# Average pooling over length 4: f32 loads without a cast, 512-row tiles, fewer buffers and a last tile in pieces

## Chip, cores and metric

The kernel runs on one core of a Trainium2 chip, with the other cores idle. The metric is the device time of one execution in microseconds (us), and a smaller time is better. The granted clock (of TensorE, which this kernel does not use) was 1.0 in every run.

## The reference

```python
x = randn(64, 256, 8192) as float32; kernel_size = 4; stride = 4
for i in range(2048):
    output[:, :, i] = mean(x[:, :, 4*i : 4*i + 4], axis=2)      # float32
```

Seen flat, 16384 rows of 8192 numbers (32 KB a row, 536.9 MB in all) become 16384 rows of 2048 numbers (8 KB a row, 134.2 MB). There is about one addition per number read, so the work is nearly all movement.

## The kernel before

```python
    P = nc.NUM_PARTITIONS
    assert num_rows % P == 0
    n_tiles = num_rows // P

    inv_k = 1.0 / float(k)

    f16 = mybir.dt.float16
    f32 = mybir.dt.float32

    with (
        nc.allow_low_precision(reason="fp16 pooling: DMA-bandwidth bound kernel"),
        tc.tile_pool(name="pin", bufs=3) as pin,
        tc.tile_pool(name="psum", bufs=3) as psum,
        tc.tile_pool(name="pout", bufs=3) as pout,
    ):
        for i in range(n_tiles):
            tin = pin.tile([P, out_len * k], f16, name="tin")
            nc.gpsimd.dma_start(
                out=tin, in_=x_flat[i * P : (i + 1) * P, 0 : out_len * k]
            )
            tsum = psum.tile([P, out_len], f16, name="tsum")
            nc.vector.reduce_sum(
                out=tsum,
                in_=tin.rearrange("p (g k) -> p g k", k=k),
                axis=mybir.AxisListType.X,
            )
            tout = pout.tile([P, out_len], f32, name="tout")
            nc.scalar.mul(tout, tsum, inv_k)
            nc.scalar.dma_start(out=out_flat[i * P : (i + 1) * P], in_=tout)

```

A tile is 128 rows, one in each partition. GpSimd issues the load; because the tile is f16 and the source f32, the transfer itself casts. VectorE sums groups of four, ScalarE multiplies by 1/4 and widens to f32, and ScalarE issues the store. Each pool has three buffers, so a load waits for the reduce three tiles before it. There are 128 such tiles; nothing is special about the first or the last. The launch code around it is left out here.

Of the kernel before, what the change touches and what calls it, by code (L numbers as in the profile page):

```python
# [1 line left out]

# [4 lines left out]


@with_exitstack
def kernel(  # L10
    ctx: ExitStack,
    tc: tile.TileContext,
    x: bass.AP,
    kernel_size: bass.AP,
    stride: bass.AP,
    out: bass.AP,
):
    nc = tc.nc

    k = int(kernel_size)  # L20
    s = int(stride)
    assert k == s, f"only kernel_size == stride supported (got {k}, {s})"

    x_flat = x.flatten_outer_dims()
    out_flat = out.flatten_outer_dims()
    num_rows, length = x_flat.shape
    out_len = out_flat.shape[1]
    assert out_len * k <= length

    P = nc.NUM_PARTITIONS  # L30
    assert num_rows % P == 0
    n_tiles = num_rows // P

    inv_k = 1.0 / float(k)

    f16 = mybir.dt.float16
    f32 = mybir.dt.float32

    with (
        nc.allow_low_precision(reason="fp16 pooling: DMA-bandwidth bound kernel"),  # L40
        tc.tile_pool(name="pin", bufs=3) as pin,
        tc.tile_pool(name="psum", bufs=3) as psum,
        tc.tile_pool(name="pout", bufs=3) as pout,
    ):
        for i in range(n_tiles):
            tin = pin.tile([P, out_len * k], f16, name="tin")
            nc.gpsimd.dma_start(  # L47
                out=tin, in_=x_flat[i * P : (i + 1) * P, 0 : out_len * k]
            )
            tsum = psum.tile([P, out_len], f16, name="tsum")  # L50
            nc.vector.reduce_sum(  # L51
                out=tsum,
                in_=tin.rearrange("p (g k) -> p g k", k=k),
                axis=mybir.AxisListType.X,
            )
            tout = pout.tile([P, out_len], f32, name="tout")
            nc.scalar.mul(tout, tsum, inv_k)  # L57
            nc.scalar.dma_start(out=out_flat[i * P : (i + 1) * P], in_=tout)


# [1 line left out]
_INS = ['x', 'kernel_size', 'stride']  # L62
_OUTS = [((64, 256, 2048), 'float32')]
#: Inputs that are plain numbers.
_NUMBERS = {'kernel_size': 4, 'stride': 4}


# [26 lines left out]
```

## Time and profile before

| | before |
|---|---|
| time, median of 13 runs | 1578.23 us (1578.12 to 1578.70) |
| span of the profiled run | 1576.4 us |
| DMA engines busy | nine tenths or more in 39 of 40 slices |
| VectorE / ScalarE busy | 71% / 16% |
| time of 512 rows (four tiles), steady | 48.81 us |

The last row is mine: from the timeline, the time from the start of a reduce to the start of the reduce four later, as the median over the run. I use 512 rows because that is one tile of the changed kernel. I call it the *step*.

These are lines of the profile page of the kernel before. Group lines give line, engine, operation, shapes and count, then busy us and mean ns of one, then the idle time of the engine before them and what ended it. Queue lines give packets, MB and share of the 16 engines' time. Issue lines give the median us from issue to landing.

```profile
span 1576.4 us, 937 instructions
...
DMA  9999999999999999999999999999999999999997
...
q0 software_dynamic: 18432, 268.44, 79.8%
q10 hardware_dynamic: 18432, 134.23, 21.0%
...
HBM read 536.87 MB, written 134.22 MB: 426 GB/s over the span
...
L51 DVE TENSOR_REDUCE tsum<-tin 128x2048 f16<-128x8192 f16 x128 | 1111.8, 8686 | 457.9 <-DMA tin<-in_x_dram 457.9
L57 ACT ACTIVATE tout<-tsum 128x2048 f32<-128x2048 f16 x128 | 244.4, 1909 | 1325.2 <-DVE tsum L51 1325.2
...
tin<-in_x_dram POOLq DMA_DIRECT2D x128, 2048.0 KB, 27.5
out_dram<-tout ACTq DMA_DIRECT2D x128, 1024.0 KB, 20.8
```

Read it from the DMA row: the engines never rest, and the two queues' shares (79.8% and 21.0%) add up to the whole span. VectorE's idle 457.9 us all end at a load. The load queue's 268.44 MB counts the f16 bytes that reach SBUF; the line "HBM read" counts the f32 bytes that leave HBM.

These are lines of the timeline of the kernel before: start us, duration us, engine, line, operation, and in brackets the idle time before it and its releaser. They show the first two reduces, two reduces four tiles apart in the steady part (one step), and the end.

```profile
13.78 8.69 DVE L51 TENSOR_REDUCE tsum<-tin 128x2048 f16<-128x8192 f16 x1 [13.78 <-DMA tin<-in_x_dram]
...
23.43 8.69 DVE L51 TENSOR_REDUCE tsum<-tin 128x2048 f16<-128x8192 f16 x1 [0.96 <-DMA tin<-in_x_dram]
...
1207.09 8.69 DVE L51 TENSOR_REDUCE tsum<-tin 128x2048 f16<-128x8192 f16 x1 [3.53 <-DMA tin<-in_x_dram]
...
1255.90 8.69 DVE L51 TENSOR_REDUCE tsum<-tin 128x2048 f16<-128x8192 f16 x1 [3.52 <-DMA tin<-in_x_dram]
...
1561.00 8.69 DVE L51 TENSOR_REDUCE tsum<-tin 128x2048 f16<-128x8192 f16 x1 [3.52 <-DMA tin<-in_x_dram]
1569.72 1.91 ACT L57 ACTIVATE tout<-tsum 128x2048 f32<-128x2048 f16 x1 [10.30 <-DVE tsum L51]
1571.66 0.34 ACTq L58 DMA_DIRECT2D out_dram<-tout  x1
```

The second tile is ready 9.65 us after the first, before any store has run: 4.194 MB of source in 9.65 us is 435 GB/s. After the last load lands at 1561.0, the reduce, the scaling and the store follow one after the other until 1576.4.

### The profile page before, as it was taken

To read this page: it belongs to the slowest core of one execution; us is meant where nothing else is said; L and a number is where in the kernel's file an instruction comes from. 1 tells how busy PE (TensorE), PEld (TensorE's weight loads), DVE (VectorE), ACT (ScalarE), POOL (GpSimd) and SP (SyncE) were. 2 spreads that over 40 slices of the span, in tenths; PEclk is the share of its full clock that TensorE was granted. 3 is DMA by queue.
4 is the path that set the end of the run, shared out by engine and by line. 5 is a ranking of instruction groups with operands and counts; after the bars stand their busy time and mean duration, and the time that the engine had idled before them with its cause. 6 is when DMAs were issued, how large, how long until landed. Compare 5 with 4: busy or idle time off the path is not lost.

```text
span 1576.4 us, 937 instructions
## 1 busy us (share of the span) xinstructions
DVE 1111.8 (71%) x128; ACT 245.7 (16%) x129; POOL 67.9 (4%) x132
## 2 busy tenths in 40 slices
DVE  5766777677766777677767776677767776677766
ACT  1111111111111111111111111111111111111111
POOL 0000000000000000000000000000000000000000
DMA  9999999999999999999999999999999999999997
GB/s 212 256 259 256 257 256 259 262 256 256 255 258 262 259 257 256 257 259 257 259 258 255 258 257 259 262 256 256 256 261 259 257 259 254 259 259 256 259 258 212
DMA packets 36871, 402.73 MB, mean 255 GB/s; under 512 B 4096, under 2 KB 4096, under 8 KB 4096
## 3 DMA queue, kind: packets, MB, share of 16 engines
q0 software_dynamic: 18432, 268.44, 79.8%
q10 hardware_dynamic: 18432, 134.23, 21.0%
q14 instruction: 7, 0.06, 0.0%
HBM read 536.87 MB, written 134.22 MB: 426 GB/s over the span
## 4 chain that ended last, share of the span: by engine, by line
DMA 75%; DVE 23%; issue 2%; ACT 0%; DVEq 0%; POOL 0%; POOLq 0%; PEldq 0%
DMA tin<-in_x_dram 75%; DVE tsum L51 23%; ACT tout L57 0%; DVEq L51 0%; POOL tin L47 0%; POOLq L89 0%; PEldq L89 0%; POOLq L47 0%
## 5 line engine op out<-in xcount | busy, mean ns | idle before, releaser
L51 DVE TENSOR_REDUCE tsum<-tin 128x2048 f16<-128x8192 f16 x128 | 1111.8, 8686 | 457.9 <-DMA tin<-in_x_dram 457.9
L57 ACT ACTIVATE tout<-tsum 128x2048 f32<-128x2048 f16 x128 | 244.4, 1909 | 1325.2 <-DVE tsum L51 1325.2
L47 POOL DMA_DIRECT2D tin<-in_x_dram x128 | 67.7, 529 | 1465.7 <-DVE tsum L51 1450.7
L57 ACT ACT_TABLE_LOAD x1 | 1.3, 1283 | 0.7 <-PEq L75 0.7
L75 POOL MEMSET const-float32-0.0<- 128x1 f32 x1 | 0.1, 99 | 0.2 <-issue 0.2
L75 POOL MEMSET const-bfloat16-1.0<- 128x1 bf16 x1 | 0.1, 102 | 0.0
L75 POOL MEMSET const-float32-1.0<- 128x1 f32 x1 | 0.1, 99 | 0.0
L75 POOL MEMSET const-uint8-127<- 128x1 uint8 x1 | 0.1, 99 | 0.0
## 6 DMA issues: line engine op xcount, KB each, us to landing
tin<-in_x_dram POOLq DMA_DIRECT2D x128, 2048.0 KB, 27.5
out_dram<-tout ACTq DMA_DIRECT2D x128, 1024.0 KB, 20.8
```

Source lines behind the costliest of these rows:

```text
L47: nc.gpsimd.dma_start(out=tin, in_=x_flat[i * P : (i + 1) * P, 0 : out_len * k])
L51: nc.vector.reduce_sum(out=tsum, in_=tin.rearrange("p (g k) -> p g k", k=k), axis=mybir.AxisListType.X,)
L57: nc.scalar.mul(tout, tsum, inv_k)
L75: nc = _bacc.Bacc("TRN2", target_bir_lowering=False, num_devices=1)
```

## The change

Its intent is to spend less on the transfers and their ends: no cast, larger transfers, a short tail. Four rows go to each partition (`(p q) l -> p (q l)`), so that a 512-row tile is loaded in two halves of 8.4 MB with 64 KB in one run per partition, and stored as one 4.2 MB transfer with 32 KB per partition. The input pool has two buffers of 64 KB per partition, the result pool two of 32 KB; the scaling is done in place. The last tile is loaded, reduced, scaled and stored by quarters, the last quarter by quarters again, and the store of the tile before it is held back behind the last loads.

```diff
-            tin = pin.tile([P, out_len * k], f16, name="tin")
-            nc.gpsimd.dma_start(
-                out=tin, in_=x_flat[i * P : (i + 1) * P, 0 : out_len * k]
-            )
...
+        with (
+            tc.tile_pool(name="pin", bufs=2) as pin,
+            tc.tile_pool(name="pq", bufs=2) as pq,
+        ):
+            for t in range(n_super):                 # 32 tiles of 512 rows, Q = 4
+                x_view = x_flat[R0 : R0 + super_rows].rearrange("(p q) l -> p (q l)", q=Q)
+                o_view = out_flat[R0 : R0 + super_rows].rearrange("(p q) m -> p (q m)", q=Q)
+                if t == n_super - 1:
...                     # by quarters j: load, reduce, scale, store; j == 3 in four pieces again
+                    continue
+                pqt = pq.tile([P, Q * out_len], f32, name="pq")
+                for h in range(Q // 2):
+                    tin = pin.tile([P, half_in], f32, name="tin")
+                    xh = x_view[:, h * half_in : (h + 1) * half_in]
...
+                    nc.sync.dma_start(out=tin, in_=xh)
+                    nc.vector.reduce_sum(out=pqt[:, h * half_out : (h + 1) * half_out],
+                                         in_=tin.rearrange("p (g k) -> p g k", k=k), axis=X)
+                nc.scalar.mul(pqt, pqt, inv_k)
+                if t == n_super - 2:
+                    deferred.append((o_view, pqt))
+                else:
+                    nc.scalar.dma_start(out=o_view, in_=pqt)
+            for o_view, pqt in deferred:
+                nc.sync.dma_start(out=o_view, in_=pqt)
```

(The lines are joined here, and a path for other shapes, which these inputs do not take, is left out.)

More of the change, by code (lines that the diff above doesn't have):

```diff
@@ L27 @@
     out_len = out_flat.shape[1]
-    assert out_len * k <= length
+    used_len = out_len * k
+    assert used_len <= length
     P = nc.NUM_PARTITIONS
+    inv_k = 1.0 / float(k)
+    f32 = mybir.dt.float32
+    X = mybir.AxisListType.X
+    Q = 4
+    super_rows = P * Q
+    fast = (
+        used_len == length
+        and num_rows % super_rows == 0
+        and out_len % 4 == 0
+        and length % (2 * k) == 0
+        and num_rows // super_rows >= 4
+    )
+    if fast:
+        n_super = num_rows // super_rows
+        half_in = 2 * length
+        half_out = 2 * out_len
+        with (
+            tc.tile_pool(name="pin", bufs=2) as pin,
+            tc.tile_pool(name="pq", bufs=2) as pq,
+        ):
+            deferred = []
+            for t in range(n_super):
+                R0 = t * super_rows
+                x_view = x_flat[R0 : R0 + super_rows].rearrange(
+                    "(p q) l -> p (q l)", q=Q
+                )
+                o_view = out_flat[R0 : R0 + super_rows].rearrange(
+                    "(p q) m -> p (q m)", q=Q
+                )
+                if t == n_super - 1:
+                    pqt = pq.tile([P, Q * out_len], f32, name="pq")
+                    for j in range(Q):
+                        if j % 2 == 0:
+                            tin2 = pin.tile([P, half_in], f32, name="tin")
+                        tinq = tin2[:, (j % 2) * length : (j % 2 + 1) * length]
+                        src = x_view[:, j * length : (j + 1) * length]
+                        oq = o_view[:, j * out_len : (j + 1) * out_len]
+                        if j < Q - 1:
+                            nc.sync.dma_start(out=tinq[:, 0:length], in_=src)
+                            nc.vector.reduce_sum(
+                                out=pqt[:, j * out_len : (j + 1) * out_len],
+                                in_=tinq[:, 0:length].rearrange(
+                                    "p (g k) -> p g k", k=k
+                                ),
+                                axis=X,
+                            )
+                            nc.scalar.mul(
+                                pqt[:, j * out_len : (j + 1) * out_len],
+                                pqt[:, j * out_len : (j + 1) * out_len],
+                                inv_k,
+                            )
+                            nc.scalar.dma_start(
+                                out=oq, in_=pqt[:, j * out_len : (j + 1) * out_len]
+                            )
+                        else:
+                            C = 4
+                            cin = length // C
+                            cout = out_len // C
+                            for c in range(C):
+                                nc.sync.dma_start(
+                                    out=tinq[:, c * cin : (c + 1) * cin],
+                                    in_=src[:, c * cin : (c + 1) * cin],
+                                )
+                                o_lo = j * out_len + c * cout
+                                o_hi = j * out_len + (c + 1) * cout
+                                nc.vector.reduce_sum(
+                                    out=pqt[:, o_lo:o_hi],
+                                    in_=tinq[:, c * cin : (c + 1) * cin].rearrange(
+                                        "p (g k) -> p g k", k=k
+                                    ),
+                                    axis=X,
+                                )
+                                nc.scalar.mul(
+                                    pqt[:, o_lo:o_hi], pqt[:, o_lo:o_hi], inv_k
+                                )
+                                nc.scalar.dma_start(
+                                    out=oq[:, c * cout : (c + 1) * cout],
+                                    in_=pqt[:, o_lo:o_hi],
+                                )
+                    continue
+                pqt = pq.tile([P, Q * out_len], f32, name="pq")
+                for h in range(Q // 2):
+                    tin = pin.tile([P, half_in], f32, name="tin")
+                    xh = x_view[:, h * half_in : (h + 1) * half_in]
+                    if t == 0 and h == 0:
+                        nc.sync.dma_start(out=tin, in_=xh)
+                    else:
+                        nc.sync.dma_start(out=tin, in_=xh)
+                    nc.vector.reduce_sum(
+                        out=pqt[:, h * half_out : (h + 1) * half_out],
+                        in_=tin.rearrange("p (g k) -> p g k", k=k),
+                        axis=X,
+                    )
+                nc.scalar.mul(pqt, pqt, inv_k)
+                if t == n_super - 2:
+                    deferred.append((o_view, pqt))
+                else:
+                    nc.scalar.dma_start(out=o_view, in_=pqt)
+            for o_view, pqt in deferred:
+                nc.sync.dma_start(out=o_view, in_=pqt)
+        return
@@ L31 @@
     assert num_rows % P == 0
     n_tiles = num_rows // P
-    inv_k = 1.0 / float(k)
-    f16 = mybir.dt.float16
-    f32 = mybir.dt.float32
     with (
-        nc.allow_low_precision(reason="fp16 pooling: DMA-bandwidth bound kernel"),
         tc.tile_pool(name="pin", bufs=3) as pin,
@@ L45 @@
         for i in range(n_tiles):
-            tin = pin.tile([P, out_len * k], f16, name="tin")
-            nc.gpsimd.dma_start(
-                out=tin, in_=x_flat[i * P : (i + 1) * P, 0 : out_len * k]
-            )
-            tsum = psum.tile([P, out_len], f16, name="tsum")
+            r0, r1 = i * P, (i + 1) * P
+            tin = pin.tile([P, used_len], f32, name="tin")
+            nc.sync.dma_start(out=tin, in_=x_flat[r0:r1, 0:used_len])
+            tsum = psum.tile([P, out_len], f32, name="tsum")
             nc.vector.reduce_sum(
@@ L53 @@
                 in_=tin.rearrange("p (g k) -> p g k", k=k),
-                axis=mybir.AxisListType.X,
+                axis=X,
             )
@@ L57 @@
             nc.scalar.mul(tout, tsum, inv_k)
-            nc.scalar.dma_start(out=out_flat[i * P : (i + 1) * P], in_=tout)
+            nc.scalar.dma_start(out=out_flat[r0:r1], in_=tout)
 _INS = ['x', 'kernel_size', 'stride']
```

## The prediction

> **What bounds the kernel now.** The 16 DMA engines. The page shows them at nine tenths or more in 39 of 40 slices; its queue part gives 79.8% of their time to loads and 21.0% to stores. VectorE is 71% busy; in the waits view VectorE waits for loads 128 times, 457.9 us. A steady tile takes 12.20 us in the timeline. The cast to f16 happens inside the load, so 4.19 MB leave HBM per tile though 2.1 MB reach SBUF; with the 1.05 MB store that is 5.24 MB in 12.20 us, 430 GB/s. Before any store ran, the second tile's data came 9.65 us after the first's (reduces start at 13.78 and 23.43): 435 GB/s of source bytes. The Trainium skill ("DMA: Bandwidth & Descriptors", Where 436 GB/s comes from) puts the ceiling at 435 GB/s; this trace agrees if source bytes are counted. So the engines are charged by HBM bytes: the cast saves them nothing.
>
> **What the change does.**
> - Drops the cast; f32 loads of 8.4 MB go from SyncE's queue instead of GpSimd's. HBM bytes stay: 536.9 MB in, 134.2 MB out. SBUF receives twice as much. I expect no change of rate.
> - Reduces: 62 of 128x16384 f32, plus a finer last tile. 8,686 ns for 8192 f16 columns is 1.06 ns a column; f32 should cost the same (the skill's "VectorE: DVE Perf Modes", tier table, caps the reduce at 1x for both): 17.2 us each. Off the chain.
> - Scaling: 31 large in-place ACTIVATEs, about 7 us each, scaled from 1,909 ns. Off the chain.
> - Stores: 4.2 MB in 32 KB rows instead of 1 MB in 8 KB rows. A store now costs 12.20-9.65 = 2.55 us (411 GB/s); larger pieces may lower it towards 2.41 us, saving up to 18 us in all.
> - Tail: now the last load lands at 1561.0 and 8.7 us of reduce, 1.9 of scaling and 3.9 of store follow, about 15 us, DMA mostly idle. After: quarter-pieces with reduce 2.3 us, scale 0.6, store about 2, while a held-back 4.2 MB store fills the DMA. Saves about 8 to 10 us.
>
> **Two buffers instead of three.** A load waits for the reduce two before it. That reduce (17.2 us) must end before the next load's data (19.3 us at 435 GB/s, no store running) do: about 2 us for semaphores and issue; stores widen it. The fastest store landed in 3.9 us against 2.4 of data: 1.5 us of latency, no bubble. If nearer 3 us, each of 31 tiles loses about 1 us.
>
> **Sum.** Loads 128 x 9.65 = 1235 us, stores 309 to 326, head about 3, tail about 3: 1550 to 1567 us. I predict **1564 us**, range **1547 to 1594**. Chances: faster by over 2%: 0.07; within 2%: 0.81; slower by over 2%: 0.12.
>
> **What would show it.** DMA at nine tenths or more in all slices, mean near 430 GB/s (the page's 255 now counts cast bytes); load queue near 79%; 48.8 us or less per 512-row tile; reduces near 17.2 us; the last load followed by about 10 us, filled by the held-back store; a chain of waits nearly all DMA.
>
> **What would make it wrong.** Writing SBUF at the full 435 GB/s could be slower; rows of one load at a 128 KB pitch could suit HBM worse; f32 reduces could run slower, closing the two-buffer slack; large stores could hold back loads; latency could open a bubble per tile.

## The result

| | before | after |
|---|---|---|
| time, median | 1578.23 us (13 runs) | 1557.73 us (7 runs, 1556.74 to 1561.30) |
| span of the profiled run | 1576.4 us | 1555.6 us |
| step (512 rows), median | 48.81 us | 48.33 us |
| reduce of 8192 columns a partition | 8.686 us | 8.61 us (half of 17.220) |

The ratio is 0.9877 (95% interval 0.9867 to 0.9887). A ratio is the mean time of one kernel's runs over that of the other's in the same rounds, so it is not quite the ratio of the medians. The class is "same" at 2%: 1.2% faster, and clear of the noise.

These are the lines of the profile page of the changed kernel that answer to those above.

```profile
span 1555.6 us, 418 instructions
...
DMA  9999999999999999999999999999999999999999
...
q1 hardware_dynamic: 10080, 541.07, 80.5%
q10 hardware_dynamic: 5328, 130.03, 19.4%
...
HBM read 536.87 MB, written 134.22 MB: 431 GB/s over the span
...
L125 DVE TENSOR_REDUCE pq<-tin 128x4096 f32<-128x16384 f32 x62 | 1067.6, 17220 | 443.4 <-DMA tin<-in_x_dram 443.4
L130 ACT ACTIVATE pq<-pq 128x8192 f32<-128x8192 f32 x31 | 217.9, 7030 | 1298.2 <-DVE pq L125 1298.2
...
out_dram<-pq ACTq DMA_DIRECT2D x30, 4096.0 KB, 32.9
...
tin<-in_x_dram SPq DMA_DIRECT2D x62, 31.1
```

It is the same picture: DMA full, VectorE waiting for loads, compute unchanged in cost. The bytes between HBM and SBUF moved at 431 GB/s in place of 426. (The load queue's 541.07 MB includes the one held-back store, which is issued from SyncE.)

These are lines of the timeline of the changed kernel in its steady part.

```profile
1418.97 17.22 DVE L125 TENSOR_REDUCE pq<-tin 128x4096 f32<-128x16384 f32 x1 [4.62 <-DMA tin<-in_x_dram]
...
1445.48 17.22 DVE L125 TENSOR_REDUCE pq<-tin 128x4096 f32<-128x16384 f32 x1 [9.28 <-DMA tin<-in_x_dram]
...
1467.32 17.22 DVE L125 TENSOR_REDUCE pq<-tin 128x4096 f32<-128x16384 f32 x1 [4.62 <-DMA tin<-in_x_dram]
```

The bracket is also the slack of the two buffers. A reduce ends, its buffer is free, and the next load into it can be issued at once; VectorE then waits 4.62 or 9.28 us for the load that is already on its way. So each load is queued that long before its predecessor lands, and the queue does not run dry.

These are lines of the stretches view at the end: start and end of the stretch, its length, busy us and instructions of VectorE, ScalarE and GpSimd, TensorE's clock, DMA share, GB/s. The kernel before:

```profile
1530.00:1561.00 31.00, 20.44 (x4) 5.73 (x3) 0.53 (x1) 1.00 1.01 266
1561.00:1570.00 9.00, 8.68 (x1) 0.28 (x1) 0.00 (x0) 1.00 0.25 106
1570.00:1576.00 6.00, 0.00 (x0) 1.63 (x1) 0.00 (x0) 1.00 0.42 175
```

The changed kernel:

```profile
1512.00:1537.00 25.00, 25.00 (x4) 10.07 (x4) 0.00 (x0) 1.00 0.99 420
1537.00:1546.00 9.00, 8.58 (x4) 4.03 (x5) 0.00 (x0) 1.00 1.05 450
1546.00:1551.00 5.00, 0.00 (x0) 0.24 (x1) 0.00 (x0) 1.00 0.92 391
1551.00:1555.60 4.60, 0.00 (x0) 0.00 (x0) 0.00 (x0) 1.00 0.58 222
```

Before, the DMA stood at a quarter for 9 us and under a half for 6 us. After, it is nearly full until about 1551. By these shares the DMA stood idle for about 10 us after the last load had landed, and for about 2.3 us after 1546 in the changed kernel: some 8 us less.

So the 20.8 us of span have two parts. The step fell by 0.48 us; over some 31 steps that is 15 us. The remaining 6 us are put down to head and tail together; that is 2 us less than the idle time that the tail alone lost, so the split is good to a few us only. The experiments ask which part of the change made which.

### The profile page after: what moved, and what is told of

The parts are those of the page before. It is cut to its first block, busy times and chain, and to the rows that moved or that the text cites. A ratio compares the mean times of both kernels' runs of the same rounds, so it can differ in the third digit from the quotient of the medians.

```text
span 1555.6 us, 418 instructions
## 1 busy us (share of the span) xinstructions
DVE 1102.2 (71%) x69; ACT 227.4 (15%) x39; POOL 0.2 (0%) x4
## 3 DMA queue, kind: packets, MB, share of 16 engines
q1 hardware_dynamic: 10080, 541.07, 80.5%
## 4 chain that ended last, share of the span: by engine, by line
DMA 63%; DVE 36%; issue 0%; DVEq 0%; ACT 0%; SPq 0%
DMA tin<-in_x_dram 63%; DVE pq L125 34%; DVE pq L75 2%; DVE pq L101 0%; DVEq L190 0%; ACT pq L108 0%; SPq L122 0%
## 5 line engine op out<-in xcount | busy, mean ns | idle before, releaser
L125 DVE TENSOR_REDUCE pq<-tin 128x4096 f32<-128x16384 f32 x62 | 1067.6, 17220 | 443.4 <-DMA tin<-in_x_dram 443.4
L130 ACT ACTIVATE pq<-pq 128x8192 f32<-128x8192 f32 x31 | 217.9, 7030 | 1298.2 <-DVE pq L125 1298.2
L75 DVE TENSOR_REDUCE pq<-tin 128x2048 f32<-128x8192 f32 x3 | 25.9, 8676 | 0.0
L101 DVE TENSOR_REDUCE pq<-tin 128x512 f32<-128x2048 f32 x4 | 8.9, 2276 | 0.0
L82 ACT ACTIVATE pq<-pq 128x2048 f32<-128x2048 f32 x3 | 5.7, 1910 | 14.9 <-DVE pq L75 14.9
## 6 DMA issues: line engine op xcount, KB each, us to landing
out_dram<-pq ACTq DMA_DIRECT2D x4, 256.0 KB, 10.8
```

What stands on the lines that cost most here:

```text
L75: nc.vector.reduce_sum(out=pqt[:, j * out_len : (j + 1) * out_len], in_=tinq[:, 0:length].rearrange("p (g k) -> p g k", k=k), axis=X,)
L82: nc.scalar.mul(pqt[:, j * out_len : (j + 1) * out_len], pqt[:, j * out_len : (j + 1) * out_len], inv_k,)
L101: nc.vector.reduce_sum(out=pqt[:, o_lo:o_hi], in_=tinq[:, c * cin : (c + 1) * cin].rearrange("p (g k) -> p g k", k=k), axis=X,)
L125: nc.vector.reduce_sum(out=pqt[:, h * half_out : (h + 1) * half_out], in_=tin.rearrange("p (g k) -> p g k", k=k), axis=X,)
L130: nc.scalar.mul(pqt, pqt, inv_k)
```

## The experiments

Twelve kernels ran. "Step" is the median step of the profiled run; times of timed runs are medians. The kernel before took 1578.17 us beside the first four, 1578.57 beside the next four and 1578.21 beside the last four, so times can be compared across them although the three groups ran on different chips.

| run | time, us | step, us |
|---|---|---|
| before | 1578.2 | 48.81 |
| after | 1557.73 | 48.33 |
| e1_f32_small: cast dropped, SyncE's queue | 1569.45 | 48.53 |
| e7_f32_pool: cast dropped, GpSimd's queue | 1570.26 | 48.54 |
| e4_before_tail: before, last tile in quarters | 1572.51 | 48.82 |
| e2_no_tail: after, without tail code | 1579.91 | 48.34 |
| e9_no_hold: after, store not held back | 1559.98 | 48.34 |
| e6_quarter_4buf: after, 4 MB loads, four buffers | 1565.87 | 48.50 |
| e3_small_stores: after, 1 MB stores | 1724.61 | not steady |
| e8_small_both: after, 1 MB stores, 2 MB loads | 1572.51 | 48.90 |

The other four move one kind of data only: l_cast 1252.34 us, l_f32 1255.30, s_1mb 327.96, s_4mb 325.59. All kernels of the table gave the correct result; these four are wrong.

### The cast alone: e1_f32_small and e7_f32_pool

Theory A was the prediction's: the engines are charged by HBM bytes, so dropping the cast is worth nothing. Theory B said that the cast and GpSimd's queue cost rate.

```diff
-            tin = pin.tile([P, out_len * k], f16, name="tin")
-            nc.gpsimd.dma_start(
+            tin = pin.tile([P, out_len * k], f32, name="tin")
+            nc.sync.dma_start(
...
-            tsum = psum.tile([P, out_len], f16, name="tsum")
+            tsum = psum.tile([P, out_len], f32, name="tsum")
```

> The kernel before with the cast dropped alone: f32 loads of 4 MB from SyncE's queue, three buffers, 1 MB stores and the old tail kept. Theory A (the engines are charged by HBM bytes, so cast and queue are worth nothing; the steady gain of the change is the larger stores): the steady tile stays at 12.20 us and the time is 1575 to 1579 us. Theory B (the cast and GpSimd's queue cost rate): the steady tile falls to about 12.08 us (a quarter of the 48.33 us of the changed kernel) and the time to about 1562 us.

It took 1569.45 us, between the two: 8.7 us were gained, ratio 0.9945 (0.9930 to 0.9959), and the step fell to 48.53 us. Theory A is wrong for the mixed case, and theory B does not get all of it. The next run puts the f32 loads back on GpSimd's queue.

```diff
-            nc.sync.dma_start(
+            nc.gpsimd.dma_start(
```

> The kernel with the cast dropped alone, but its f32 loads issued from GpSimd's queue as before. The run with SyncE's queue took 1569.45 us, the kernel before 1578.2. If the cast itself was the cost beside stores: about 1570 us and 48.6 us per 512 rows. If GpSimd's queue was: about 1578 us and 48.85 us.

It took 1570.26 us with a step of 48.54 us, ratio 0.9950 (0.9933 to 0.9966). So the steady gain is the cast's, not the queue's. SyncE's queue is worth another 0.8 us, and that is at the head: the first reduce starts at 13.11 us with it and at 13.89 us without. (Both edits also make the sums f32. The reduces and the scalings take 8,686 and 1,909 ns either way, so that is not where the gain comes from.) These two reduces of e1 are one step apart:

```profile
1273.32 8.69 DVE L51 TENSOR_REDUCE tsum<-tin 128x2048 f32<-128x8192 f32 x1 [3.44 <-DMA tin<-in_x_dram]
...
1321.85 8.69 DVE L51 TENSOR_REDUCE tsum<-tin 128x2048 f32<-128x8192 f32 x1 [3.43 <-DMA tin<-in_x_dram]
```

### Loads and stores by themselves: l_cast, l_f32, s_1mb, s_4mb

Each of these keeps the pools of the kernel before and drops everything but one kind of transfer (the loads keep one store at the end). Here with the cast; l_f32 has `f32` and `nc.sync` in those places:

```diff
         for i in range(n_tiles):
             tin = pin.tile([P, out_len * k], f16, name="tin")
             nc.gpsimd.dma_start(out=tin, in_=x_flat[...])
-            ... reduce, scale, store
+        tout = pout.tile([P, out_len], f32, name="tout")
+        nc.scalar.mul(tout, tin[:, 0:out_len], inv_k)
+        nc.scalar.dma_start(out=out_flat[0:P], in_=tout)
```

The stores alone, with Q = 1 (s_1mb) or Q = 4 (s_4mb):

```diff
-            ... load, reduce, scale, store
+        for t in range(n_tiles // Q):
+            tout = pout.tile([P, Q * out_len], f32, name="tout")
+            nc.vector.memset(tout, 0.0)
+            nc.scalar.dma_start(
+                out=out_flat[t * P * Q : (t + 1) * P * Q].rearrange("(p q) m -> p (q m)", q=Q),
+                in_=tout,
+            )
```

> Loads alone, f32 to f16 with the cast from GpSimd's queue, three buffers, one store at the end, result wrong on purpose. Theory A: 9.65 us a load, about 1235 us of loads and about 1245 us in all. If the engines were charged by the bytes that reach SBUF it would be half of that.

> Loads alone, f32 kept, from SyncE's queue, same sizes and buffers, result wrong on purpose. Theory A: the same as with the cast, 9.65 to 9.68 us a load, 1243 to 1248 us in all. Theory B (cast and software queue cost rate): clearly shorter than the run with the cast, by about 15 us.

> Stores alone, 128 of 1 MB with 8 KB rows from tiles set to zero, result wrong on purpose. If small pieces cost by themselves: 2.55 us each, about 330 us. If they cost only among loads: about 2.41 us each, 310 to 315 us.

> Stores alone, 32 of 4 MB with 32 KB rows from tiles set to zero, result wrong on purpose. About 2.41 to 2.43 us per MB-tile, 310 to 315 us; the difference to the run with 1 MB stores is what the piece size costs by itself, expected about 15 us.

The loads took 1252.34 us with the cast and 1255.30 us without: alone, the cast costs nothing that these show (it is even 3 us the shorter). (Both are at least 7 us above what I expected: the rate at the head, 9.65 us a load, does not quite hold.) These are the queue lines of the DMA view between 200 and 1200 us, first with the cast:

```profile
q0 software_dynamic: 14864, 216.54, 101.6%
```

and without it:

```profile
q1 hardware_dynamic: 14831, 431.99, 100.4%
```

In the same 1000 us the cast delivered 216.54 MB of f16 (433.1 MB of source) and the plain load 431.99 MB of f32. So the engines are indeed charged by HBM bytes when only loads run. The plain load takes 4.194/0.432 = 9.71 us per 128 rows; with the cast, the issues in the timeline stand 9.69 us apart.

The stores alone took 327.96 and 325.59 us in all, but the second run begins its first store only at 9.4 us, after a longer memset, so the totals hide the difference. These are the sums of the DMA view between 50 and 250 us, first with 1 MB stores (8 KB rows), then with 4 MB stores (32 KB rows):

```profile
DMA packets 11505, 83.78 MB, mean 419 GB/s; under 512 B 1279, under 2 KB 1279, under 8 KB 1279
```

```profile
DMA packets 2950, 86.18 MB, mean 431 GB/s; under 512 B 320, under 2 KB 320, under 8 KB 320
```

That is 2.50 and 2.43 us per 128 rows. Small stores do cost by themselves: 0.07 us, 9 us over 128 tiles, less than the 15 us that I had expected.

Now the parts can be summed, four tiles to a step:

| | sum of the parts | measured step |
|---|---|---|
| before: cast load + 8 KB rows | 4 x (9.69 + 2.50) = 48.76 | 48.81 |
| e1: plain load + 8 KB rows | 4 x (9.71 + 2.50) = 48.84 | 48.53 |
| e6: plain 4 MB load + 32 KB rows | 4 x (9.71 + 2.43) = 48.56 | 48.50 |

With the cast, loads and stores add up in full. Without it, loads and small stores together take 0.31 us less than their sum. By this sum, the gain of dropping the cast is overlap, which appears only where both directions run together. (The parts come from one look each, so the sum is an argument; that the gain is there, and is the cast's, e1 and e7 show.) Why the engines can overlap plain transfers a little and not casting ones, no run here shows.

### Large stores or large loads: e6_quarter_4buf

```diff
-            tc.tile_pool(name="pin", bufs=2) as pin,
+            tc.tile_pool(name="pin", bufs=4) as pin,
...
-                for h in range(Q // 2):
-                    tin = pin.tile([P, half_in], f32, name="tin")
-                    xh = x_view[:, h * half_in : (h + 1) * half_in]
+                for h in range(Q):
+                    tin = pin.tile([P, length], f32, name="tin")
+                    xh = x_view[:, h * length : (h + 1) * length]
...                     # and the reduce writes out_len columns at a time
```

(The last tile's quarters each get a buffer of their own too.)

> The changed kernel with f32 loads of 4 MB (32 KB rows) into four buffers in place of 8 MB (64 KB rows) into two: the same SBUF, more loads ahead; stores and tail kept. If two buffers cost nothing and only the bytes and the store pieces count: the period of 512 rows stays at 48.3 to 48.4 us and the time within 4 us of the changed kernel, 1554 to 1562 us. If two large buffers open a bubble: at least 10 us faster than the changed kernel. If the 64 KB load rows are what gained: the period goes back to 48.6 us and the time to about 1565 us.

It took 1565.87 us (1564.13 to 1567.10), ratio 0.9921 (0.9906 to 0.9936), with a step of 48.50 us. The time is that of the third case of the expectation; the step lies between the first and the third. These two reduces of e6 are one step apart:

```profile
1204.56 8.69 DVE L123 TENSOR_REDUCE pq<-tin 128x2048 f32<-128x8192 f32 x1 [10.68 <-DMA tin<-in_x_dram]
...
1253.06 8.69 DVE L123 TENSOR_REDUCE pq<-tin 128x2048 f32<-128x8192 f32 x1 [10.70 <-DMA tin<-in_x_dram]
```

The difference to e1's step, 48.53, is 0.03 us although the stores are four times as large. The difference to the changed kernel, 48.33, is 0.17 us although only the form of the loads differs. So the large stores by themselves gave next to nothing, and the part of the steady gain that is not the cast's came with the loads in halves of 8.4 MB. (The large stores are needed all the same: with small ones, these loads lose far more, as e3 below shows.) The loads differ in three ways at once (row length, transfer size, number of buffers), and which of the three counts stays open; no run has the large loads by themselves. Four buffers of half the size gave no gain: two were enough. The 8 us between the two kernels are no measure of the loads alone. The profiled run of e6 has a stretch of steps of 49.2 to 50.2 us, which the median hides: its mean step from the third to the 31st tile is 48.76 us, against 48.36 in the changed kernel and 48.58 in e1. And its tail is worse: in its last 11.3 us the DMA share is 0.30, in the last 4.6 us of the changed kernel 0.58.

### The tail: e4_before_tail, e2_no_tail, e9_no_hold

e4_before_tail gives the kernel before a last tile in quarters:

```diff
-        for i in range(n_tiles):
+        for i in range(n_tiles - 1):
...
...                     # i, cin, cout and the three tiles of the last 128 rows
+        for c in range(4):
+            a, b = slice(c * cin, (c + 1) * cin), slice(c * cout, (c + 1) * cout)
+            nc.gpsimd.dma_start(out=tin[:, a], in_=x_flat[i * P : (i + 1) * P, a])
+            nc.vector.reduce_sum(out=tsum[:, b], in_=tin[:, a].rearrange("p (g k) -> p g k", k=k), axis=X)
+            nc.scalar.mul(tout[:, b], tsum[:, b], inv_k)
+            nc.scalar.dma_start(out=out_flat[i * P : (i + 1) * P, b], in_=tout[:, b])
```

> The kernel before with only its last tile cut into four quarter-length pieces (load, reduce, scale, store each), cast kept. Expected from its own durations: 6.4 us less of reduce, 1.3 less of scaling and about 1.5 less of store after the last load, so 1568 to 1572 us with a steady tile of 12.20 us. If the idle DMA at the end is not what the tail costs, it stays above 1575 us.

It took 1572.51 us, 5.7 less than before, ratio 0.9964 (0.9949 to 0.9978), at an unchanged step of 48.82 us. That is just outside the range that I gave, and in its direction: VectorE had work left over when the last quarters came (its four short reduces run back to back from 1557.07), so the saving was smaller than the sum of durations.

e2_no_tail takes the tail code out of the changed kernel:

```diff
-                if t == n_super - 1:
+                if False:
...
-                if t == n_super - 2:
+                if False:
```

> The changed kernel with its special last tile and held-back store taken out: the last 512 rows are handled like the others. Both theories: steady period unchanged at 48.33 us. After the last load come 17.2 us of reduce, 7.0 of scaling and about 11 of store, and the store of the tile before covers only the first few us of it, so about 20 us of idle DMA are added: 1572 to 1582 us, which would eat the whole gain of the change. If the tail is worth little, it stays below 1563 us.

It took 1579.91 us, ratio 1.0014 (0.9997 to 1.0030), with the step of the changed kernel (48.34). These are its last stretches:

```profile
1541.00:1550.00 9.00, 8.42 (x1) 0.00 (x0) 0.00 (x0) 1.00 0.14 58
1550.00:1566.00 16.00, 8.80 (x1) 7.03 (x1) 0.00 (x0) 1.00 0.00 0
1566.00:1577.80 11.80, 0.00 (x0) 0.00 (x0) 0.00 (x0) 1.00 0.83 355
```

The DMA does nothing for 16 us while 17.2 us of reduce and 7.0 us of scaling finish, and then a 4.2 MB store runs alone. A four times larger tile makes a longer tail, and that alone eats the whole gain. The tail code is worth 22 us here, 1557.73 against 1579.91.

e9_no_hold keeps the pieces and drops only the holding back, by the second of the two edits above.

> The changed kernel with the last tile still in pieces but the store of the tile before it no longer held back behind the last loads (issued from ScalarE's queue like the others). If holding back matters: that store takes part of the DMA from the last loads, the last pieces come later, and the time is 3 to 10 us longer than the changed kernel's. If cutting the last tile is what counts and VectorE's backlog covers the loads: within 2 us of it.

It took 1559.98 us (1559.69 to 1565.53): 2.2 us above the changed kernel by the medians, less than the 4.6 us between the changed kernel's own fastest and slowest run, so the timing does not settle it. The traces suggest why little came of it; that of e9 is of its slowest run, 5.5 us above its median, so they do not settle it either. Without holding back, the last pieces of the load come later, and VectorE waits for them (7.9 us in all before its last four reduces; 0.0 in the changed kernel). With it, the last small stores queue among the large one and land after 10.8 us in place of 5.0.

### Who gets the DMA: e3_small_stores and e8_small_both

```diff
-                    nc.scalar.dma_start(out=o_view, in_=pqt)
+                    for j in range(Q):
+                        nc.scalar.dma_start(
+                            out=o_view[:, j * out_len : (j + 1) * out_len],
+                            in_=pqt[:, j * out_len : (j + 1) * out_len],
+                        )
```

> The changed kernel with each 4 MB store cut into four of 1 MB with 8 KB rows, loads and tail kept. Theory A (store size makes the steady gain): the period goes from 48.33 back to about 48.8 us and the time to about 1572 us. Theory B (cast and queue): the period stays at 48.33 us and the time at 1557 to 1561 us.

It took 1724.61 us, ratio 1.0928 (1.0912 to 1.0944). Neither theory had this. This is the group line of its reduces:

```profile
L125 DVE TENSOR_REDUCE pq<-tin 128x4096 f32<-128x16384 f32 x62 | 1066.2, 17217 | 611.0 <-DMA out_dram<-pq 443.7 <-DMA tin<-in_x_dram 167.3
```

VectorE now waits 443.7 us for stores: the result buffer of two tiles before is not written out yet. The queue lines of the DMA view between 716 and 730 us, while loads and stores both run, tell why (packets, MB, share):

```profile
q1 hardware_dynamic: 80, 5.24, 94.5%
q10 hardware_dynamic: 78, 0.64, 10.8%
```

This is the same view of the changed kernel between 120 and 136 us:

```profile
q1 hardware_dynamic: 71, 4.65, 67.6%
q10 hardware_dynamic: 72, 2.36, 34.1%
```

In both, the queues move packet for packet, 80 to 78 and 71 to 72. (Where one load ends and the next begins, more store packets get through: 107 to 48 in e3 between 730 and 737 us.) The packets differ: 65 KB of load and 33 KB of store in the changed kernel, 65 KB and 8 KB here. So the stores' share of the bytes falls from a third to a ninth, and they need a fifth on average. The stores fall behind, the reduces stop for want of a result buffer, both input buffers stay full, and no load can be issued. Between 780 and 800 us the stretches view has the DMA at 0.57. The Trainium skill says it in "DMA: Bandwidth & Descriptors", Queues, rings and completion order: each engine goes round the queues that have work, packet by packet.

The next run tests that against the idea that 8 KB rows at a 32 KB pitch are simply slow: it cuts the loads as well.

```diff
...                     # in place of the one load; the stores are cut as in e3
+                    for c in range(4):
+                        a, b = c * half_in // 4, (c + 1) * half_in // 4
+                        nc.sync.dma_start(out=tin[:, a:b], in_=xh[:, a:b])
```

> The run with 1 MB stores of 8 KB rows, which took 1724.6 us, with each 8 MB load also cut into four, so that load rows are 16 KB. Theory (the DMA engines take turns between the two queues piece by piece, so the queue with larger pieces gets the larger share; at 64 to 8 KB the stores starve and the result buffers are not free in time): the ratio is 2 to 1 again as in the changed kernel, the waits of VectorE for stores vanish, the period is 48.6 to 49.2 us and the time 1565 to 1585 us. Rival (8 KB rows at a 32 KB pitch are slow among loads by themselves): it stays above 1680 us.

It took 1572.51 us, ratio 0.9965 (0.9950 to 0.9980), and no wait of VectorE for a store is left. This is its DMA view between 709 and 725 us:

```profile
q1 hardware_dynamic: 316, 4.51, 65.8%
q10 hardware_dynamic: 321, 2.37, 35.0%
```

The stores are the same as in e3; the loads' packets are now 16 KB, the ratio is 2 to 1 again, and 152 us are back. Small pieces on both sides cost 0.57 us a step against the changed kernel (48.90 to 48.33); the times differ by 14.8 us.

## Why the prediction was right, and where it was not

- **The bound and the total: right.** The DMA was and stayed the bound, and 1557.73 us lies in the range of 1547 to 1594, 6 us under the point. "Within 2%" was right.
- **The bytes: right alone, wrong in the mix.** "So the engines are charged by HBM bytes: the cast saves them nothing" holds for loads alone (216.54 MB of f16 and 431.99 MB of f32 in the same time). "I expect no change of rate" failed: dropping the cast alone took 8.0 us off (e7); by the sum of the parts, that is because plain loads and stores overlapped a little and casting loads did not. A term of the sum that stood at zero was about 8 us.
- **The stores: the wrong term.** "Larger pieces may lower it towards 2.41 us, saving up to 18 us in all": stores alone went from 2.50 to 2.43 us, and beside plain loads of 4 MB the larger store changed the step by only 0.03 us (e6 against e1). The 2.55 us that the prediction gave a store of the kernel before is too much because it is a difference to the rate at the head: a load alone takes 9.69 us with the cast, not 9.65. The 0.17 us of step, some 5 us, that remained came with the loads in 8.4 MB halves, which the prediction gave no gain at all.
- **The tail: right in direction, its size not settled.** I said 8 to 10 us. The idle time of the DMA at the end fell by some 8 us, but only about 6 us of span are left for head and tail, and e4's simpler cut of the kernel before gave 5.7 us. What I did not say is that the larger tile would first have cost some 20 us (e2), so that the tail code is what keeps the rest of the change from being worth nothing.
- **Two buffers: right.** No bubble: loads are queued 4.6 and 9.3 us before they are needed, and four buffers of half the size were not faster (e6).
- **The reduces: right.** 17,220 ns for 16384 f32 columns against 17.2 us predicted. The Trainium skill's "VectorE: DVE Perf Modes", tier table, caps the reduce at 1x, its slowest mode, for both types; the trace agrees, since e1's reduces of 8192 f32 columns take 8,686 ns, as the f16 ones did.
- **The ceiling: right.** The skill's 435 GB/s ("DMA: Bandwidth & Descriptors", Where 436 GB/s comes from, where it is the limit of the SBUF ports) is what the undisturbed loads at the head reach (9.65 us per 4.194 MB); 432 GB/s is what they keep up alone, and 434 GB/s is what the changed kernel moves in both directions together (20.97 MB in 48.33 us). The gain was small because before it already stood at 430.

The prediction's sum came out near the truth partly by luck, because errors offset each other. It gave the cast no gain and the stores too much. And it put 128 loads at 9.65 us where they take 9.71 alone, some 8 us too little, but left out that loads and stores overlap: the parts of a step, 4 x (9.71 + 2.43) = 48.56 us, are 0.23 us more than the 48.33 measured, about 7 us over 32 steps. (That is an estimate: the 9.71 is of 4 MB loads.)

Put together from differences of times: the cast 8.0 us, the queue 0.8 us, and 11.7 us for large loads, stores and tail together (e1 to after), of which the step explains about 6 us; the rest is put down to head and tail. Open stay three things: what about the large loads counts, why the cast prevents the overlap, and what the occasional longer steps are (up to 49.37 us in the profile of the kernel before, up to 50.2 in that of e6), and whether they are what spreads the changed kernel's runs over 4.6 us.

## What to carry to other kernels

When the DMA engines are full, first divide the HBM bytes by the time: at 430 of some 435 GB/s, only the ends and a per cent or so of overlap were left to gain here, and the cast in the load neither saved time nor was quite free. Two queues shared the engines packet for packet here (80 to 78, 71 to 72), so the size of the pieces on each queue set its share; keep the store's share by bytes at least at what it needs, or its buffers stall the whole kernel. A larger tile brings a longer tail (36 us from the last load to the end in e2, 15 us before), and must be cut into pieces at the end.

## What the Trainium skill lacked or had wrong

- "DMA: Bandwidth & Descriptors", Rules for kernel authors, says only where to issue a cast. Missing is its price: none in loads alone (433 GB/s of source bytes against 432), and 0.28 us a step (48.81 to 48.53), 8 us in all, where stores run beside it.
- The same page, Queues, rings and completion order, has the turn-taking by packets but not its consequence: bytes are shared in the ratio of packet sizes (2.0 to 1 and 8.2 to 1 measured), which made one kernel 9.3% slower.
- The same page, SWDGE vs HWDGE vs iDMA, gives a packet as "≤4096 B preferably", for descriptors that GpSimd builds; what the profile counts as packets carried 29 KB on average in GpSimd's own loads (e7: 18,432 packets, 536.88 MB) and 65 KB in SyncE's (71 packets, 4.65 MB). Whether the two mean the same by a packet, no run here shows.
- The same page's table of measured bandwidth is for loads from GpSimd's queue. Missing for this chip are stores: 419 GB/s with 8 KB rows and 431 GB/s with 32 KB rows, both alone.
